# A hybrid encoder step: an empty step in the mixers' schedule, and two up-projection operands queued behind the out-projection

## The chip, the cores and the metric

The kernel runs on one core of one Trainium2 chip. The core has five engines, each with its own in-order queue: TensorE (PE) multiplies matrices, VectorE (DVE) and ScalarE (ACT) do elementwise work, GpSimd (POOL) does small elementwise work, and SyncE (SP) issues transfers. The metric is the device time of one execution in microseconds (us). The time before is the median of three runs, 1380.83 us (1377.18 to 1381.84).

## The reference

One inference step of one layer: a token mixer with three groups of heads in parallel (GLA, HGRN2 and mLSTM), then a causal convolutional feed-forward network, each with RMS norms and a residual. There are 1024 new prompt frames and 32 frames of a running stream, width 1024, feed-forward width 2816, all in float32.

```python
def run_layer(x, st, ffn_buf, p):
    xn = rms_norm(x, g_mix_pre)
    proj = xn @ w_in                               # queries, keys, values, gates of 16 heads
    o_a, s_gla = gated_linear_scan(q, k, v, log_a, s_gla)     # 6 heads
    o_b, s_hg = gated_linear_scan(q2, k2, v2, log_f, s_hg)    # 5 heads
    h, (c, n, m) = mlstm_scan(q3, k3, v3, log_fm, ig, c, n, m)  # 5 heads
    cat = concat(norm(o_a) * silu(.), norm(o_b) * silu(.), norm(h) * sigmoid(.))
    x = x + rms_norm(cat @ w_out, g_mix_post)
    up = causal_dwconv(rms_norm(x, g_ffn_pre) @ w_up, ffn_buf)
    gate, val = split(up)
    return x + rms_norm((gelu(gate) * val) @ w_down, g_ffn_post)
```

`gated_linear_scan` is S_t = diag(a_t) S_{t-1} + k_t v_t^T, o_t = S_t^T q_t, computed in blocks of 64 frames: scores within a block, and a state carried from block to block.

## The kernel before

The frames are worked on in nine units: units 0 to 7 are 128 prompt frames each, unit 8 is the 32 frames of the running stream. The in-projection takes them in three groups: units 0 to 2, units 3 to 5, and units 6, 7 and 8. Every product of float32 operands is three products of rounded halves: an operand is cast on ACT to its high half (name ending in h), DVE subtracts it to get the low half (ending in l), and `mm3` (L101 to L103) multiplies high by high, low by high and high by low.

Nothing in the program is ordered by hand in the end. A planner goes through the traced instructions with a model of the engines, and puts on each engine's queue the instruction that is ready, the one traced first ahead of the others. `tc.high_priority(offset=n)` lets instructions count as traced n places earlier. `tc.issue_after(ins)` makes every instruction traced inside it stand behind `ins` on the queue of the same engine. The order in which the Python generators are advanced therefore sets the priorities.

There are two strands. The main strand is the in-projection of a group (`inproj`, 38 steps: three of norm transposes and first values, feature tiles, then 21 steps of value and gate blocks of about 24 matmuls each) or, at the end, the out-projection (`pipeline` over the units 0, 1, 2, 3, 8, 4, 5). The side strand is the `mixer` of the units of the group before (units 8, 6 and 7, in this order, beside the out-projection). `merge` advances the two: after main step i, side steps are taken until (i+1)·nside/nmain of them have been done (integer division).

A mixer has nine steps, each ended by a `yield`: loads (eleven transfers into buffers of which there is mostly one); decays, scaled queries and keys; three steps of a pair of score levels each, the scores going from PSUM (sc) into the matrix P on DVE (`put`, L805), the last of these also with the state update (`states`, S, L902 and L903); the outputs (og and oh, 88 small matmuls for a full unit: P times v and the scaled queries qz times the states, then the memory update C); the output norm (`finish`, L987 to L992); the memory outputs om and oi, whose PSUM buffers are the same two as those of og and oh; and the norm of those, the gate and the store of the unit's 1024 columns (cat). `NMIX` sets how many side steps the merges count on: 3·NMIX − 6 beside the second group, 3·NMIX beside the third, 3·NMIX + 2 over 26 main steps of the out-projection.

At the end, the out-projection of units 6 and 7 overlaps the first up-projection block. `outproj` transposes a unit's columns (ctp, L1074), casts the halves of 512 columns to ch and cl (L1078, L1079; three buffers each), multiplies them with the weights (zp), takes z out of PSUM (L1101, L1102), norms it and adds the residual (L1147 to L1164), and transposes it again for the up-projection (fxt, L1178). ch waits for one of its three buffers, so the second half of unit 7 waits for the first products of unit 6. The up-projection multiplies 2x2 blocks by a scheme with seven products. Its column operands come from the loaded tile xg in `col_operands` (L1211): B21, B11 at once, and B12, B22 and their sums T1 to T4 after unit 5's columns have come. `halves` (L1216) makes each operand's two halves (L1221 on ACT, L1222 on DVE). The tiles of B21 and B11 lie in memory that the mixers have used. `kept` is a dictionary in which instructions are kept by name for later `issue_after`.

Of the kernel before, what the change touches and what calls it, by code (L numbers as in the profile page):

```python
# [8 lines left out]
F32 = mybir.dt.float32  # L9
# [4 lines left out]
ALU = mybir.AluOpType  # L14
# [77 lines left out]
def body(ctx: ExitStack, tc: tile.TileContext, a: dict):  # L92
    nc = tc.nc
    act, dve, pool, pe, sp = nc.scalar, nc.vector, nc.gpsimd, nc.tensor, nc.sync
# [620 lines left out]
    def soon(fn, *args, **kw):  # L715
        with tc.issue_after(line[0].ins) if line[0] else ExitStack():
            line[0] = fn(*args, **kw)  # L717

    def mixer(u, g, ci0):
# [3 lines left out]
        cl = chunks[0][1]  # L723
# [52 lines left out]
        with ExitStack() as behind:  # L776
            if halves:

                for ins in (kwi[0], halves[1]):
                    behind.enter_context(tc.issue_after(ins.ins))  # L780
            spread(dve, qz, lambda r, fs, psl: dve.tensor_tensor(qz[r, psl, :n], q4[r, fs, :], eb4[r, fs, :],
                                                                 op=ALU.mult), n)
# [3 lines left out]
        with tc.issue_after(outs[1].ins) if outs else ExitStack():  # L786
            dve.tensor_tensor(khf.rearrange("p (m c) -> p m c", c=cl), b5[:, :, cl - 1:cl].broadcast_to([128, 4 * nch, cl]),
                              b5, op=ALU.subtract)
# [55 lines left out]
        def scores(sc, c, L, Q, at):  # L844
            for j in (3, 0, 1, 2):
                for (o, m) in chunks:
                    for hf in range(2):
                        f, q0, q1, p0 = HALVES[hf][j]
                        r = slice(64 * hf, 64 * hf + 64)
                        mm = c if c == levels[0] else m  # L850
                        soon(pe.matmul, sc[o:o + mm, p0:p0 + q1 - q0, at:at + m // 2], L[r, f, o:o + mm],
                             Q[r, q0:q1, o // 2:(o + m) // 2], start=True, stop=True)
# [6 lines left out]
        def keys():  # L859
            for f0 in (0, 2):  # L860
                kps = small(2, 128)
                for f in (f0, f0 + 1):
                    soon(pe.transpose, kps[:n, f - f0, :], khf[:, f * n:f * n + n], ident)
                for ch, (o, m) in enumerate(chunks):
                    with tc.high_priority(offset=AHEAD):
                        act.copy(kt2[o:o + m, ch, 128 * f0:128 * f0 + 256], kps[o:o + m].rearrange("p f n -> p (f n)"))
# [4 lines left out]
        def memory_scores():  # L871
            sm = psm.tile([128, 6, 64], F32, tag="o", name=f"sm{u}", bufs=2)
            for f in range(3):
                rows, hs = (128, slice(2 * f, 2 * f + 2)) if f < 2 else (64, slice(4, 5))
                for (o, m) in chunks:
                    soon(pe.matmul, sm[o:o + m, hs, :m], mk[:rows, f, o:o + m], mqz[:rows, hs, o:o + m], start=True, stop=True)
            kp = small(4, 64)
            for f in range(2):
                soon(pe.transpose, kp[:n, 2 * f:2 * f + 2, :].rearrange("p h d -> p (h d)"), mk[:, f, :], ident)
            soon(pe.transpose, sm[:n, 5, :], mk[:64, 2, :], ident[:64, :64])  # L880
            for (h0, h1, kp) in ((0, 4, kp), (4, 5, sm[:, 5:6])):
                for ch, (o, m) in enumerate(chunks):
                    kwi[0] = dve.tensor_tensor(kw2[o:o + m, ch, h0:h1], kp[o:o + m, :h1 - h0],
                                               cols[o:o + m, 96 + h0:96 + h1].unsqueeze(2).broadcast_to([m, h1 - h0, 64]), op=ALU.mult)
            dve.tensor_tensor(w3, w3, sm[:n, :5, :cl], op=ALU.mult)
# [39 lines left out]
        for l0 in range(0, len(levels), 2):  # L925
            pair = [operands(c, i) for i, c in enumerate(levels[l0:l0 + 2])]
            last_pair = pair[-1][0] == levels[-1]
            if last_pair:
                z = mx.tile([128, 512], F32, tag="x", name=f"x{u}_0", bufs=NX)
                dve.tensor_tensor(z[:, :4 * n], q4.rearrange("p f n -> p (f n)"), k4.rearrange("p f n -> p (f n)"), op=ALU.mult)  # L930
            if l0 == 2:
                act.copy(mqz[0:64, 0:5:2, :n], mq[0:64, :, :])
                act.copy(mqz[64:128, 1:4:2, :n], mq[64:128, 0:2, :])
                dve.tensor_tensor(w3, ab3[:n], cols[:n, 0:5].unsqueeze(2).broadcast_to([n, 5, cl]), op=ALU.add)
                dve.tensor_tensor(w3, w3, caus[:n, :cl].unsqueeze(1).broadcast_to([n, 5, cl]), op=ALU.min)
                act.activation(w3, w3, AF.Exp)
            sct = psm.tile([128, 1024], F32, tag="sc", name=f"sc{u}_{l0}", bufs=1)
            sc = sct[:, :11 * SCW].rearrange("p (h s) -> p h s", s=SCW)
            line[0] = None
            for i in reversed(range(len(pair))):  # L940
                scores(sc, *pair[i], i * (cl // 2))
            sd = sct[:, 11 * SCW:11 * SCW + 11]
            if l0 == 0:
                keys()
            elif l0 == 2:
                memory_scores()
            if last_pair:
                for f in range(4):
                    soon(pe.matmul, sd[:n], z[:, f * n:f * n + n], of_head[:, f, :], start=f == 0, stop=f == 3)
                si = states()  # L950
            for i, (c, L, Q) in enumerate(pair):
                at = i * (cl // 2)
                if c == levels[0]:
                    for (o, m) in chunks:
                        act.copy(P[o:o + c, :, c:2 * c], sc[o:o + c, :, at:at + c])
                else:
                    put(c, sc[:n, :, at:at + cl // 2])
            if last_pair:
                put(0, sd[:n].unsqueeze(2).broadcast_to([n, 11, cl]))
            yield  # L960

        og = psm.tile([128, 6, 64], F32, tag="o", name=f"og{u}", bufs=2)
        oh = psm.tile([128, 5, 64], F32, tag="o", name=f"oh{u}", bufs=2)
# [90 lines left out]
    def outproj(p2, W, u):  # L1054
# [9 lines left out]
        for hf in range(2):  # L1064
            if u < 7 or u == 8:
                ps = psb.tile([128, 4, 128], F32, tag="big", name=f"ctp{u}{hf}")
            else:

                if not hf:
                    both = psm.tile([128, 2, 4, 128], F32, tag="sc", name="ctp7", bufs=1)  # L1070
                ps = both[:, hf]
            for k in range(4):
                c = 512 * hf + 128 * k
                pe.transpose(ps[:, k, :n], ct[:n, c:c + 128], ident[:n, :n])  # L1074
            ch = p2.tile([128, 4, 128], F32R, tag="ch", name=f"ch{u}{hf}", bufs=3)
            cl = p2.tile([128, 4, 128], F32R, tag="cl", name=f"cl{u}{hf}", bufs=3)
            with tc.high_priority(offset=AHEAD):
                ins = (act.copy(ch[:, :, :n], ps[:, :, :n]),  # L1078
                       dve.tensor_tensor(cl[:, :, :n], ps[:, :, :n], ch[:, :, :n].bitcast(F32), op=ALU.subtract))  # L1079
            if u == RING[0]:  # L1080
                halves[:] = ins
            chs += [(ch[:, k, :n], cl[:, k, :n]) for k in range(4)]
            if u in RING:
                yield
# [84 lines left out]
        else:  # L1169
            s = u > 5  # L1170
# [18 lines left out]
    upper, jks, kept = [], [], {}  # L1189
# [21 lines left out]
    def col_operands(pool_, q, s, between=lambda: None):  # L1211

        n = SUBS[s][1]
        res = {}

        def halves(name, src):  # L1216
            p = pool_[name in ("T2", "T3")]
            h = p.tile([128, 4, n], F32R, name=f"{name}h{s}")
            l = p.tile([128, 4, n], F32R, name=f"{name}l{s}")
            res[name] = h, l  # L1220
            act.copy(h, src)  # L1221
            return dve.tensor_tensor(l, src, h.bitcast(F32), op=ALU.subtract)  # L1222

        halves("B21", q["B21"])
        halves("B11", q["B11"])
        between()
        t1 = q["B11"]
        dve.tensor_tensor(t1, q["B12"], t1, op=ALU.subtract)
        halves("T1", t1)
        halves("B22", q["B22"])  # L1230
        t3, t2, t4 = q["B12"], q["B22"], q["B21"]
        dve.tensor_tensor(t3, q["B22"], t3, op=ALU.subtract)
        dve.tensor_tensor(t2, t2, t1, op=ALU.subtract)
        dve.tensor_tensor(t4, t2, t4, op=ALU.subtract)
        with ExitStack() as behind:
            if s == 0:
                behind.enter_context(tc.issue_after(kept["jk"].ins))
            halves("T2", t2)
        ins = halves("T4", t4)
        between()  # L1240
        with tc.issue_after(ins.ins):
            halves("T3", t3)
        return res
# [447 lines left out]
        return chain_of(*[mixer(u, g, c) for (u, c) in us[-1:] + us[:-1]]) if us[-1][0] == 8 else \  # L1691
            chain_of(*[mixer(u, g, c) for (u, c) in us])

    NMIX, NIN = 11, 12 + 2 + 24

    for g in range(3):
        xs_ = norm_tiles(g)
# [18 lines left out]
    n0, n1 = SUBS[0][1], SUBS[1][1]  # L1716
    smp = DEC // 2
    firsts = [outproj(p2, wo, u) for u in RING]
    merge(pipeline(firsts), 26, 3 * NMIX + 2)
    pump(1000)  # L1720
# [10 lines left out]
    p4s, p5s, p6s, p7s, p8s, p9s, pxs, phs, late = (ExitStack() for _ in range(9))  # L1731
# [213 lines left out]
```

## Time and profile before

| | before |
|---|---|
| median of three runs | 1380.83 us |
| the profiled execution, its time | 1379.03 us |
| the profiled execution, its span in the trace | 1377.3 us |
| mean granted TensorE clock | 0.982 |
| PE busy | 1313.3 us (95%) |
| DVE busy | 1031.8 us (75%) |
| ACT busy | 703.9 us (51%) |
| POOL busy | 325.6 us (24%) |

The span is divided into about 110 us of in-projection with no mixer beside it, the in-projections of the second and third group with the mixers of the group before to about 510 us, the out-projection with the last three mixers to about 680 us, the up-projection to about 1140 us, and the down-projection.

How to read the rows: a row of the timeline has the start and the duration in us, the engine, the line of the kernel, the operation, the output and the inputs by the program's names, their shapes, the number of merged instructions, and in brackets how long the engine was idle before and what ended the idle time. `SPq` and `POOLq` are queues that issue transfers. The granted clock is the share of TensorE's full clock.

### The profile page before, as it was taken

What the parts mean: (1) busy time and instruction counts of PE and PEld (TensorE: products, weight loads), DVE (VectorE), ACT (ScalarE), POOL (GpSimd) and SP (SyncE); (2) the same over time, 40 slices, a digit from 0 to 9 for tenths busy, and PEclk for the clock granted to TensorE, in tenths of its full rate; (3) what the DMA queues carried; (4) which work ended last, traced back from release to release, by engine and by line L of the source; (5) the groups of instructions that cost most, each with busy time, mean ns of one, the idle gap of its engine ahead of it and who ended that gap; (6) DMA issues with size and microseconds to landing.
All of it is one profiled execution on the core that took longest, in us unless ns stands there. A gap on an engine that the chain in (4) does not pass through costs nothing.

```text
span 1377.3 us, 29190 instructions
## 1 busy us (share of the span) xinstructions
PE 1313.3 (95%) x11472; PEld 1194.7 (87%) x11472; DVE 1031.8 (75%) x1916; ACT 703.9 (51%) x1368; POOL 325.6 (24%) x529
## 2 busy tenths in 40 slices
PE   6999999998998989997989999999999999999996
PEld 5999989998887877866879999999999997678885
DVE  4786469668597577796778888888888875499566
ACT  4555556554474554443575455455555445454552
POOL 5532403145122064133111112121121110010005
PEclk9999999999999999999999999999999999999998
DMA  9599869785888844534323565645474239744435
GB/s 343 203 321 359 288 235 299 267 281 188 273 256 309 303 147 161 155 114 151 110 77 110 170 165 135 163 129 163 111 182 126 81 114 390 290 153 136 146 106 123
DMA packets 125825, 269.72 MB, mean 196 GB/s; under 512 B 24007, under 2 KB 59367, under 8 KB 125607
## 3 DMA queue, kind: packets, MB, share of 16 engines
q1 hardware_dynamic: 111959, 245.43, 52.2%
q0 software_dynamic: 8928, 18.09, 7.2%
q10 hardware_dynamic: 4800, 4.33, 0.9%
q8 instruction: 90, 1.47, 0.4%
q14 instruction: 48, 0.39, 0.1%
HBM read 206.72 MB, written 86.18 MB: 213 GB/s over the span
## 4 chain that ended last, share of the span: by engine, by line
PE 72%; DVE 11%; DMA 7%; ACT 5%; issue 2%; POOL 2%; SPq 1%; ACTq 0%; DVEq 0%; POOLq 0%
PE pux L103 5%; PE pux L101 5%; PE pux L102 5%; PE puw L101 3%; PE puw L102 3%; PE puw L103 3%; PE pv L101 3%; PE pv L103 3%; PE q L101 3%; PE pv L102 3%; PE q L102 3%; PE q L103 3%; PE x L101 2%; PE x L102 2%; PE x L103 2%
## 5 line engine op out<-in xcount | busy, mean ns | idle before, releaser
L1368 DVE SCALAR_TENSOR_TENSOR y<-uu,fconv_sb,y 128x1060 f32<-128x1060 f32 x88 | 116.2, 1320 | 37.3 <-ACT y L1366 36.9
L1304 ACT COPY c<-pux 128x272 f32<-128x272 f32 (+1 forms) x132 | 49.4, 376 | 48.3 <-PE pux L103 47.6
L101 PE MATMUL zp<-woh,ch 128*128 128x512 f32 (+1 forms) x144 | 60.5, 422 | 4.8 <-ACT ch L1078 2.8
L101 PE MATMUL pv<-wt_0h,xh 128*128 128x256 f32 (+2 forms) x195 | 57.6, 296 | 5.2 <-ACT xh L321 2.8
L103 PE MATMUL zp<-woh,cl 128*128 128x512 f32 (+1 forms) x144 | 59.0, 410 | 1.9 <-DVE cl L1079 1.9
L1366 ACT ACTIVATE y<-uu,fconv_sb 128x1060 f32<-128x1060 f32 x44 | 56.0, 1273 | 7.9 <-POOL uu L1362 6.8
L102 PE MATMUL zp<-wol,ch 128*128 128x512 f32 (+1 forms) x144 | 58.9, 409 | 0.0
L1365 POOL COPY fhalo<-uu 128x2 f32<-128x2 f32 x44 | 16.5, 376 | 178.9 <-DVE uu L1309 178.7
L103 PE MATMUL pv<-wt_0h,xl 128*128 128x256 f32 (+2 forms) x195 | 56.0, 287 | 0.2 <-DVE xl L322 0.2
L102 PE MATMUL pv<-wt_0l,xh 128*128 128x256 f32 (+2 forms) x195 | 56.0, 287 | 0.1
L103 PE MATMUL pv<-wt_1h,xl 128*128 128x256 f32 (+2 forms) x195 | 56.1, 288 | 0.0
L101 PE MATMUL pv<-wt_1h,xh 128*128 128x256 f32 (+2 forms) x195 | 55.9, 287 | 0.0
L102 PE MATMUL pv<-wt_1l,xh 128*128 128x256 f32 (+2 forms) x195 | 55.7, 286 | 0.0
L1544 POOL TENSOR_TENSOR gss<-gss 128x1 f32<-128x1 f32 (+1 forms) x9 | 8.4, 930 | 185.1 <-ACT gjk L1537 185.1
L220 POOL TENSOR_SCALAR hrs<-hss 128x5 f32<-128x5 f32 (+3 forms) x27 | 9.7, 358 | 175.4 <-DVE hss L988 174.7
L805 DVE COPY_PREDICATED P<-masks_sb,sc 128x352 f32<-128x352 int32 (+3 forms) x53 | 37.8, 714 | 11.6 <-PE sc L717 10.9
L101 PEld LDWEIGHTS pv<-wt_0h,xh 128*128 128x128 f32 (+1 forms) x195 | 36.8, 189 | 7.1 <-ACT xh L321 3.5
L431 POOL TENSOR_TENSOR vg<-vth,gh 128x256 f32<-128x256 f32 (+1 forms) x36 | 29.1, 810 | 58.5 <-DVE vth L427 36.6
L221 POOL TENSOR_TENSOR hrs<-hrs,mhalf 128x5 f32<-128x5 f32 (+3 forms) x27 | 39.7, 1471 | 2.2
L827 ACT ACTIVATE x<-x 128x256 f32<-128x256 f32 (+1 forms) x44 | 17.9, 406 | 43.3 <-DVE x L825 36.1
L101 PEld LDWEIGHTS zp<-woh,ch 128*128 128x128 f32 (+1 forms) x144 | 27.4, 190 | 12.5 <-ACT ch L1078 3.0
L992 POOL TENSOR_TENSOR cat<-cat,gt 128x320 f32<-128x320 f32 (+3 forms) x27 | 31.7, 1174 | 26.4 <-DVE cat L990 26.3
(1714 smaller groups left out, 5351.3 us busy)
## 6 DMA issues: line engine op xcount, KB each, us to landing
wrP<-in_w_dn SPq DMA_DIRECT2D x27, 512.0 KB, 4.0
h_d<-y SPq DMA_DIRECT2D x22, 530.0 KB, 3.2
ht<-h_d SPq DMA_DIRECT2D x22, 530.0 KB, 9.8
wt_0r<-in_w_tok SPq DMA_DIRECT2D x21, 512.0 KB, 7.1
wt_1r<-in_w_tok SPq DMA_DIRECT2D x21, 512.0 KB, 6.1
ws_d<-in_w_dn POOLq DMA_DIRECT2D x20, 512.0 KB, 9.1
wrP<-ws_d SPq DMA_DIRECT2D x20, 512.0 KB, 3.9
wt_0l<-lt_d SPq DMA_DIRECT2D x14, 512.0 KB, 5.7
```

The costliest lines, as they stand in the source:

```text
L101: pe.matmul(ps, lh[0], rh[0], start=first, stop=False, **kw)
L102: pe.matmul(ps, lh[0], rh[1], start=False, stop=False, **kw)
L103: return pe.matmul(ps, lh[1], rh[0], start=False, stop=last, **kw)
L221: pool.tensor_tensor(out, out, mhalf[:n, :cols], op=ALU.pow)
L431: pool.tensor_tensor(o[:n], th[:n], gh[:n, c0:c0 + 256], op=ALU.mult)
L805: dve.copy_predicated(dst, mk.broadcast_to([n, 11, *mk.shape[2:]]), src)
L827: act.activation(xv[:, :, 0, :], xv[:, :, 0, :], AF.Exp, scale=-1.0)
L992: pool.tensor_tensor(cat[:n, c0:c0 + 64 * nh], cat[:n, c0:c0 + 64 * nh], gt[:n, c0:c0 + 64 * nh], op=ALU.mult)
L1304: kept[name] = act.copy(t, ps)
L1365: behind["POOL"] = pool.tensor_copy(fhalo[:, j, :], u[:, NCOL - 2:NCOL])
L1366: act.activation(y, u, AF.Identity, scale=fconv[:, j, 2:3], bias=fconv[:, j, 3:4])
L1368: dve.scalar_tensor_tensor(y, uu[i][:, s:s + NCOL], fconv[:, j, s:s + 1], y, op0=ALU.mult, op1=ALU.add)
```

## The change

The mixer gets a tenth step with nothing in it, between the last pair of score levels with the state update and the outputs; `NMIX` goes from 11 to 12, so that the side steps in the three merges become 30 (of 30), 36 (for 30) and 38 (for 30) in place of 27 (of 27), 33 (for 27) and 35 (for 27). And in `col_operands` for the first column half (s = 0), the two casts and the two subtractions that make the halves of B21 and B11 are put behind the cast and the subtraction of the last half of unit 7's out-projection operands, on ACT and DVE.

```diff
@@ mixer
             if last_pair:
                 put(0, sd[:n].unsqueeze(2).broadcast_to([n, 11, cl]))
             yield
+        yield
 
         og = psm.tile([128, 6, 64], F32, tag="o", name=f"og{u}", bufs=2)
@@ outproj
             if u == RING[0]:
                 halves[:] = ins
+            if u == 7:
+                kept["ch"], kept["cl"] = ins
             chs += [(ch[:, k, :n], cl[:, k, :n]) for k in range(4)]
@@ col_operands
             res[name] = h, l
-            act.copy(h, src)
-            return dve.tensor_tensor(l, src, h.bitcast(F32), op=ALU.subtract)
+            with ExitStack() as late:
+                if s == 0 and name in ("B21", "B11"):
+                    late.enter_context(tc.issue_after(kept["ch"].ins))
+                    late.enter_context(tc.issue_after(kept["cl"].ins))
+                act.copy(h, src)
+                return dve.tensor_tensor(l, src, h.bitcast(F32), op=ALU.subtract)
@@ body
-    NMIX, NIN = 11, 12 + 2 + 24
+    NMIX, NIN = 12, 12 + 2 + 24
```

The loop over the two halves of unit 7 keeps the instructions of the second half, which overwrite those of the first.

## The prediction

> **What bounds the kernel now.** I read the page's busy times first, then TensorE's own waits, then the stretches around those waits, and last the order of the engines where the out-projection hands over to the up-projection.
>
> ```profile
> PE 1313.3 (95%) x11472; PEld 1194.7 (87%) x11472; DVE 1031.8 (75%) x1916; ACT 703.9 (51%) x1368; POOL 325.6 (24%) x529
> ```
>
> TensorE (PE) is busy 1313.3 of 1377.3 us, and it has enough independent products to work on at almost every moment. So the time can move by two things only: idle time of PE, and stretches in which PE runs at a lower granted clock. The change removes no arithmetic. PE's waits, by who ended them (total, times, longest):
>
> ```profile
> PE og L717 <- DVE P L805: 5.2, 3, 2.8
> PE pb L455 <- ACT vf L468: 3.9, 2, 3.2
> PE zp L101 <- ACT ch L1078: 2.8, 1, 2.8
> PE om L717 <- DVE cat L990: 2.7, 2, 1.8
> PE zp L103 <- DVE cl L1079: 1.9, 1, 1.9
> ```
>
> The first and fourth rows are a mixer's output products (og) waiting for the score matrix P, and its memory outputs (om) waiting for a PSUM buffer that the output normalisation frees. The third and fifth rows are one place, the start of unit 6's out-projection. No row of that view has PE waiting for a DMA. The clock is in the stretches (columns: stretch, length, busy time and count of PE, weight loads, DVE, ACT, POOL, then granted clock, DMA share, GB/s):
>
> ```profile
> 190.00:200.00 10.00, 10.00 (x142) 8.58 (x141) 6.28 (x10) 6.95 (x9) 0.00 (x0) 0.83 0.67 249
> 312.00:322.00 10.00, 7.19 (x126) 6.80 (x126) 7.66 (x13) 3.32 (x9) 3.52 (x6) 0.83 0.29 100
> 436.00:448.00 12.00, 7.89 (x58) 7.00 (x57) 10.26 (x26) 6.12 (x14) 6.09 (x6) 0.72 0.91 352
> 654.00:659.00 5.00, 5.00 (x13) 3.95 (x13) 4.46 (x7) 1.63 (x3) 1.00 (x2) 0.52 0.51 137
> 645.00:667.20 22.20, 17.03 (x74) 13.35 (x73) 16.73 (x23) 10.30 (x18) 5.31 (x7) 0.85 0.41 123
> ```
>
> A stall therefore costs its idle time and, often, half-clock work beside it: 10 us at 0.83 is 1.7 us of work lost, 5 us at 0.52 is 2.4 us.
>
> **Part 2 of the change, the handover.** These are the rows of ACT, DVE, POOL and PE around it, in each engine's order (start, duration, what, idle before it and its releaser):
>
> ```profile
> 647.30 1.10 ACT L1221 CAST B21h<-xg 128x1088 fp32r<-128x1088 f32 x1 [3.56 <-POOL cat L992]
> 648.31 0.59 ACT L1101 ACTIVATE z<-zp 128x512 f32<-128x512 f32 x1
> 648.89 1.09 ACT L1221 CAST B11h<-xg 128x1088 fp32r<-128x1088 f32 x1
> 650.36 1.57 ACT L1078 CAST ch<-ctp 128x512 fp32r<-128x512 f32 x3
> 646.25 1.28 DVE L1183 TENSOR_TENSOR z<-fxt,gcols_sb 128x512 f32<-128x512 f32 x2
> 648.44 1.29 DVE L1222 TENSOR_TENSOR B21l<-xg,B21h 128x1088 fp32r<-128x1088 f32 x1 [0.91 <-ACT B21h L1221]
> 650.01 1.29 DVE L1222 TENSOR_TENSOR B11l<-xg,B11h 128x1088 fp32r<-128x1088 f32 x1 [0.28 <-ACT B11h L1221]
> 651.75 1.28 DVE L1154 SCALAR_TENSOR_TENSOR z<-z,oss,gm 128x1024 f32<-128x1024 f32 x1 [0.44 <-POOL oss L221]
> 652.95 1.88 DVE L1079 TENSOR_TENSOR cl<-ctp,ch 128x512 fp32r<-128x512 f32 x3
> 646.41 0.86 POOL L992 TENSOR_TENSOR cat<-cat,gt 128x320 f32<-128x320 f32 x1 [0.60 <-DVE cat L990]
> 649.07 0.71 POOL L1147 TENSOR_TENSOR oss<-oss 128x1 f32<-128x1 f32 x1 [1.80 <-ACT z L1101]
> 650.15 1.56 POOL L221 TENSOR_TENSOR oss<-oss,mhalf 128x1 f32<-128x1 f32 x1
> 644.82 0.40 PE L103 MATMUL zp<-woh,cl 128*128 128x512 f32 x1
> 646.99 1.26 PE L1074 MATMUL ctp<-ident,ct 128*128 128x128 f32 x8 [0.46 <-DVE z L1183]
> 651.01 0.50 PE L101 MATMUL zp<-woh,ch 128*128 128x512 f32 x1 [2.76 <-ACT ch L1078]
> 653.69 0.80 PE L103 MATMUL zp<-woh,cl 128*128 128x512 f32 x1 [1.94 <-DVE cl L1079]
> ```
>
> B21h stands at the head of ACT's queue and waits 3.56 us, until POOL has finished the last mixer (its tile lies in the memory that the mixers give back). Behind it stand the two leave operations of unit 5 (z, L1101 and L1102) and the three casts ch, for which the transposes end at 646.99 + 1.26 = 648.25. The edit takes the two casts (1.10 and 1.09 us) from in front of ch, and the two subtractions (1.29 each) from in front of cl on DVE. It issues no new instruction.
>
> Without them the leave operations go at about 645.2, when unit 5's products end, and unit 6's first cast runs while its second half is still transposed: PE's 2.76 us go. For cl there are two orders. If cl is put ahead of L1154 (cl is traced with priority), DVE is free at 646.25 + 1.28 = 647.5 and the first cl needed ends at about 649: PE starts the third product there instead of at 653.69, a gain of 4.7, all of 2.76 + 1.94. If L1154 stays ahead, it waits for POOL's chain (649.07 to 651.71, so 2.64 us), which can start only after L992 ends at 647.27: 649.9, plus 1.28 for L1154, plus two casts of 1.88/3: third product at 652.5, gain 1.2. I take 4.0, nearer the priority. The clock term, 2.4 us in 654–659, goes with the wait or stays with it: I take 2.0 (0 to 2.4).
>
> What is late next: B21 and B11 must follow the last halves of unit 7's operands.
>
> ```profile
> 662.38 0.59 ACT L1078 CAST ch<-ctp 128x512 fp32r<-128x512 f32 x1 [3.23 <-PE ctp L1074]
> 663.00 0.69 DVE L1079 TENSOR_TENSOR cl<-ctp,ch 128x512 fp32r<-128x512 f32 x1 [1.23 <-ACT ch L1078]
> 667.16 0.29 PE L101 MATMUL puy<-B21h,A_0h 128*128 128x272 f32 x1
> 668.84 0.48 PE L101 MATMUL zp<-woh,ch 128*128 128x512 f32 x1
> 679.61 0.39 PE L103 MATMUL zp<-woh,cl 128*128 128x512 f32 x1
> ```
>
> These last halves are ready at 663.69. Behind them the casts end at 664.1 and 665.2, the subtractions at about 665.3 and 666.6, just before PE wants them at 667.16. All of that moves earlier together, since ch waits for unit 6's first products. Queued behind the two delayed casts on ACT, and the two subtractions on DVE, can be weight halves S_0 of the first up-projection block; PE needs them for products after the ones with B21 and B11. DVE has 22.2 − 16.7 = 5.5 us idle in 645–667.2 for the 2.6 us, and behind 667.16 lies the cover: unit 7's 48 products, 668.84 to 679.61, 0.23 us each, 11 us. I cost it at nothing. Without that cover it costs the two subtractions, 2.6 us. Part 2: −4.0 − 2.0 = **−6.0** (−7.1 to +1.4).
>
> **Part 1, the empty step.** It issues nothing. It only changes which step of the main work each mixer step is traced behind, which is the planner's priority. Counting (i+1)·n/38 for the two in-projections and (i+1)·n/26 for the out-projection, with n from 27, 33, 35 to 30, 36, 38: the last score pair with the states comes one main step earlier in units 0, 1, 2 and 4; the outputs come one step later in units 2, 3, 5 and 7; unit 7's outputs no longer share a step with its states. Besides, these move by one: earlier unit 0's first pair, unit 1's loads and second pair, and unit 2's second step; later the output norms of units 0, 5, 6, 7, the memory outputs of 1, 4, 5, 8, the closing of unit 4, the loads of unit 5 and the second step of unit 7. An output step carries its products og and oh, the memory update's products and six DVE operations; an output norm two ACT, four DVE and six POOL instructions; a load step eleven SP transfers; unit 7's outputs one more, moved past the load of unit 5's rows. What stands on the path is only what PE waits for:
>
> ```profile
> 311.74 1.75 DVE L307 SCALAR_TENSOR_TENSOR x<-x,rs,gx 32x1024 f32<-32x1024 f32 x1 [0.70 <-POOL rs L221]
> 313.42 2.86 DVE L805 COPY_PREDICATED P<-masks_sb,sc 128x352 f32<-128x352 int32 x3
> 316.33 0.92 PE L717 MATMUL og<-v,P 64*64 64x64 f32 x24 [2.81 <-DVE P L805]
> 429.85 0.33 PE L717 MATMUL og<-v,P 64*64 64x64 f32 x4 [1.45 <-DVE P L805]
> 443.88 1.35 PE L717 MATMUL om<-vm,w 64*64 64x65 f32 x20 [0.89 <-DVE cat L990]
> 626.54 0.91 PE L717 MATMUL og<-v,P 64*64 64x64 f32 x24 [0.93 <-DVE P L805]
> 632.35 0.80 PE L717 MATMUL om<-vm,w 64*64 64x65 f32 x20 [1.83 <-DVE cat L990]
> ```
>
> Unit 2 (316.33): P is late because the three L307 operations of the next group stand ahead of it on DVE. With the states a step earlier, P is traced before them; with the outputs a step later, PE gets a step of 24 products in front of og. A 128x512 product takes 0.23 us, so 24 of half the columns are an estimated 2.8 us, as long as the wait of 2.81. I take 4.0 of 2.81 + 1.7 (clock). Unit 4: 1.45 + 0.89, both with a step more of room, I take 1.5. Unit 7: 0.93 has more room, but 1.83 is a wait for the norm, which itself moves a step later; I take 0.5. Against it, new waits. The nearest row is the longest wait of PE in the same stage, pb for vf, 3.2 us, with 12 × 0.28 = 3.4 us of clock in 436–448, so 0 to 6.6; I take 2. Part 1: −4.0 − 1.5 − 0.5 + 2.0 = **−4.0** (−9 to +7).
>
> Sum: −10.0. The profiled execution took 1379.03 us (span 1377.3 and 1.7 around it), so 1369.0; the median shown, 1380.83, is 1.8 higher, so **1370.8**.
>
> **The rivals.** *The clock stays.* In 190–200 PE is busy the whole 10 us and still has 0.83: there the states' and scores' small products run, and no gap. If the half-clock stretches come from those and not from the waits, they stay, and 2.0 + 1.7 is not gained: 1374.5. The row of 312–322 speaks against it, with its gap of 2.81. The Trainium skill (TensorE: Matmul & The Clock Gate, "Why this matters for your kernels") asks only that no idle gap exceed about 3 us; by it no gap of 2.81 or 2.76 costs clock, and the sum would also be 1374.5. The trace does not agree with it at 190–200, where the clock falls without a gap.
>
> *Nothing but a trade.* The planner orders everything anew; what units 2, 4 and 7 gain comes back elsewhere, and cl stays behind L1154: −1.2, so 1379.6. For it: the waits are spread over the whole mixer stage. Against it: the handover's cause is local.
>
> *Slower: v is held longer, and the weights with it.*
>
> ```profile
> SPq L739 <- PE oh L717: 32.9, 6, 9.5
> ```
>
> v has one buffer, and its next load waits in SP's queue for oh, up to 9.5 us already; the in-projection's weight loads stand behind it. Outputs a step later (units 2, 3, 5, each with a successor) hold that queue an estimated 2.8 us longer each. It decides once the hold exceeds the lead of the weight loads. Then PE loses 3 × (2.8 + 1.7) = 13.5 instead of gaining 4.0, and keeps part 2's 6.0: +7.5, so 1388.3. Against it: PE now waits for no DMA.
>
> **How the numbers follow.** Forecast 0.50, clock stays 0.13, trade 0.12, slower 0.25. A run of this kernel tells 0.3% from no change, 4.1 us: 1376.7 to 1385.0. Faster: 0.50 + 0.13 + 0.02 of the trade = 0.65; same: 0.10 + 0.02 of the slower case = 0.12; slower 0.23. The forecast's own range is 1361 to 1377; with most of the slower case, 1360 to 1389.
>
> **What would show it.** Right: no B21h ahead of ch at the handover, the two zp waits below 1.5 us together, 654–659 near clock 1.0; og's wait for P gone in unit 2; puy without a wait for B21l. Wrong: a new PE wait over 2 us for a DMA or for P in the mixer stage, or puy waiting for B21l after unit 7's products.

## The result, and the profile after

| | before | after |
|---|---|---|
| median | 1378.82 us (15 runs, 1373.37 to 1385.35) | 1374.32 us (15 runs, 1371.81 to 1378.15) |
| ratio after / before | | 0.9968 (0.9954 to 0.9982) |
| the profiled execution, its time | 1379.03 us | 1371.81 us |
| mean granted clock of the profiled execution | 0.982 | 0.987 |

The ratio is worth 0.0032 × 1378.82 = 4.4 us (2.5 to 6.3). The two profiled executions lie 7.2 us apart, because the one of after is the fastest of its 15 runs; so stretches are compared below, and not whole spans.

The changed kernel's page (span, then busy time, share and instructions of each engine):

```profile
span 1370.0 us, 29214 instructions
PE 1309.2 (96%) x11472; PEld 1191.7 (87%) x11472; DVE 1030.3 (75%) x1916; ACT 704.6 (51%) x1368; POOL 329.9 (24%) x529
```

The counts are those of before: nothing was added or removed. TensorE's waits in the changed kernel:

```profile
PE pb L455 <- ACT vf L468: 4.4, 1, 4.4
...
PE pv L101 <- DVE vth L427: 3.6, 2, 2.9
PE om L717 <- DVE cat L991: 3.2, 2, 1.8
...
PE og L717 <- DVE P L805: 2.1, 2, 1.1
...
PE zp L103 <- DVE cl L1080: 1.3, 1, 1.3
```

The wait of og for P fell from 5.2 to 2.1 us, and zp's for ch from 2.8 to 0.2; but pb waits 4.4 in place of 3.9, and pv for vth 3.6, with a longest of 2.9. The handover in the changed kernel, as the timeline has it for PE, ACT, DVE and POOL:

```profile
642.92 0.60 PE L1075 MATMUL ctp<-ident,cat 128*128 128x128 f32 x4
645.31 0.50 PE L101 MATMUL zp<-woh,ch 128*128 128x512 f32 x1 [0.24 <-ACT ch L1079]
647.30 0.50 PE L103 MATMUL zp<-woh,cl 128*128 128x512 f32 x1 [1.26 <-DVE cl L1080]
659.99 0.29 PE L101 MATMUL puy<-B21h,A_0h 128*128 128x272 f32 x1
660.11 1.04 PE L1181 MATMUL fxt<-ident,z 128*128 128x128 f32 x8
671.90 0.29 PE L102 MATMUL puy<-B21l,A_0h 128*128 128x272 f32 x1
...
642.25 0.60 ACT L1104 ACTIVATE z<-zp 128x512 f32<-128x512 f32 x1 [1.52 <-PE zp L103]
644.67 1.56 ACT L1079 CAST ch<-ctp 128x512 fp32r<-128x512 f32 x3 [1.11 <-PE ctp L1075]
656.81 1.11 ACT L1228 CAST B21h<-xg 128x1088 fp32r<-128x1088 f32 x1
...
645.36 1.28 DVE L1157 SCALAR_TENSOR_TENSOR z<-z,oss,gm 128x1024 f32<-128x1024 f32 x1 [0.84 <-POOL oss L221]
646.56 1.28 DVE L1080 TENSOR_TENSOR cl<-ctp,ch 128x512 fp32r<-128x512 f32 x2
659.16 1.28 DVE L1229 TENSOR_TENSOR B11l<-xg,B11h 128x1088 fp32r<-128x1088 f32 x1
...
644.22 0.20 POOL L1150 TENSOR_TENSOR oss<-oss 128x1 f32<-128x1 f32 x1
644.78 0.55 POOL L221 TENSOR_TENSOR oss<-oss,mhalf 128x1 f32<-128x1 f32 x1
```

Lines have moved by one to three (L1078 is L1079, L1154 is L1157). ACT goes from the leave operations straight to ch; B21h comes 12 us later, and the first puy products take B21h and B21l without a wait. Unit 5's norm multiply, L1157, still stands ahead of cl on DVE, and cl's wait is 1.26 us. The two waits together are 0.24 + 1.26 = 1.50, where they were 2.76 + 1.94 = 4.70.

The clock of the changed kernel from the start of unit 6's transposes (ctp) to the transposes of z (fxt), and over the first 5 us from the first low product on (columns as in the prediction's windows):

```profile
642.90:660.10 17.20, 15.25 (x67) 11.92 (x66) 14.55 (x20) 9.38 (x17) 2.49 (x6) 0.90 0.51 154
647.30:652.30 5.00, 5.00 (x15) 3.96 (x16) 4.16 (x6) 2.81 (x5) 0.35 (x2) 0.66 0.94 301
```

The start of the transposes in the kernel before, and its clock over the 5 us from the first low product on:

```profile
645.93 0.60 PE L1074 MATMUL ctp<-ident,cat 128*128 128x128 f32 x4
653.69:658.69 5.00, 5.00 (x12) 3.98 (x13) 4.77 (x7) 1.42 (x4) 0.69 (x2) 0.50 0.44 113
```

To compare the same work in both, take the stretch from the start of unit 6's transposes to the first product puy: 645.93 to 667.16 before, which is 21.23 us, and 642.92 to 659.99 after, which is 17.07. So this place became 4.2 us shorter. Of these, 3.2 are waits. From the first low product to puy there is no idle time of PE in either kernel, and that part fell from 13.47 to 12.69 us: 0.8 of clock. The remaining 0.2 is the transposes, 1.26 and 1.09 us.

### The profile page after: what moved, and what is told of

It reads as the page before. It is cut to its first block, busy times and chain, and to the rows that moved or that the text cites. A ratio compares the mean times of both kernels' runs of the same rounds, so it can differ in the third digit from the quotient of the medians.

```text
span 1370.0 us, 29214 instructions
## 1 busy us (share of the span) xinstructions
PE 1309.2 (96%) x11472; PEld 1191.7 (87%) x11472; DVE 1030.3 (75%) x1916; ACT 704.6 (51%) x1368; POOL 329.9 (24%) x529
## 4 chain that ended last, share of the span: by engine, by line
PE 65%; DVE 13%; DMA 8%; ACT 7%; issue 3%; POOL 3%; SPq 1%; ACTq 0%; DVEq 0%; POOLq 0%
PE pux L103 5%; PE pux L102 5%; PE pux L101 5%; PE puw L102 3%; PE puw L103 3%; PE puw L101 3%; PE q L101 3%; PE q L102 3%; PE q L103 3%; PE pv L101 3%; PE pv L103 2%; PE x L101 2%; DMA qkb<-qkb_d 2%; PE pv L102 2%; PE x L102 2%
## 5 line engine op out<-in xcount | busy, mean ns | idle before, releaser
L1369 POOL COPY uu<-uu 128x2 f32<-128x2 f32 x44 | 31.4, 714 | 43.6 <-DVE uu L1316 42.7
L221 POOL TENSOR_TENSOR hrs<-hrs,mhalf 128x5 f32<-128x5 f32 (+3 forms) x27 | 39.3, 1454 | 2.3
L102 PEld LDWEIGHTS pv<-wt_0l,xh 128*128 128x128 f32 (+1 forms) x195 | 36.9, 189 | 0.6 <-POOL wt_0l L110 0.5
```

Of the source, the lines that this page charges most:

```text
L102: pe.matmul(ps, lh[0], rh[1], start=False, stop=False, **kw)
L221: pool.tensor_tensor(out, out, mhalf[:n, :cols], op=ALU.pow)
L1369: pool.tensor_copy(u[:, GAP_P:GAP_P + 2], u[:, GAP_S - 2:GAP_S])
```

## The experiments

Two theories were tested first. One: the handover carries the whole gain, and the empty step only moves waits about. Its rival: both parts gain, the step about as much as the handover. All kernels ran in two sets of five rounds, each set on one chip beside the kernel before (1378.68 us there in the first set, 29 runs; 1379.74 in the second, 18 runs).

**The empty step alone.**

```diff
+        yield
-    NMIX, NIN = 11, 12 + 2 + 24
+    NMIX, NIN = 12, 12 + 2 + 24
```

> The empty step with NMIX 12 alone; B21 and B11 are queued as before. Theory A (the handover carries the gain, the empty step mostly trades waits): 0 to -3 us against before, ratio 0.998 to 1.000, and at the start of unit 6's products the two waits for ch and cl are there as before, 4 to 5 us together. Theory B (the step carries the gain): -4 us or more, ratio at most 0.997. Theory C (the two only work together): slower than before.

Measured: 1378.82 us (12 runs), ratio 1.0003 (0.9988 to 1.0018). TensorE's waits between 150 us and the handover (150 to 642 us), first in the kernel before:

```profile
PE og L717 <- DVE P L805: 5.2, 3, 2.8
...
PE pv L101 <- DVE vth L427: 0.8, 2, 0.6
PE oi L717 <- DVE cat L990: 0.3, 1, 0.3
```

and with the step alone:

```profile
PE pv L101 <- DVE vth L427: 3.8, 1, 3.8
PE om L717 <- DVE cat L991: 3.1, 2, 1.8
PE oi L717 <- DVE cat L991: 2.9, 3, 1.1
...
PE og L717 <- DVE P L805: 0.9, 1, 0.9
...
PE mi L717 <- ACT kt L866: 0.6, 2, 0.4
```

og's wait for P falls by 4.3 us, as the change means it to. In its place pv's wait for vth grows from 0.8 to 3.8 us, and oi's for the norm from 0.3 to 2.9: the fifteen rows of each view add up to 25.0 us before and 26.0 with the step. The handover is as it was (zp waits 2.77 and 1.82), and PE comes to it at the same time: unit 6's transposes start at 646.04, against 645.93 before. The step is worth nothing that can be measured, though it does just what it says at og. A single profile tells such waits only roughly: the changed kernel has the same mixers, and by the same view its waits for P are 2.1 and not 0.9, its wait for vth 2.9, and its sum 25.7.

**The queueing alone.**

```diff
+            if u == 7:
+                kept["ch"], kept["cl"] = ins
...
+                if s == 0 and name in ("B21", "B11"):
+                    late.enter_context(tc.issue_after(kept["ch"].ins))
+                    late.enter_context(tc.issue_after(kept["cl"].ins))
```

> The queueing of B21 and B11 behind unit 7's last operands alone; nine mixer steps and NMIX 11 as before. Theory A: -4 to -5 us, ratio 0.996 to 0.997; the mixer stage up to 640 us has before's waits, 2.8 us before og at unit 2 among them; the two waits at unit 6 together are 1.5 us, and from there to the end the trace runs 4 to 5 us earlier than before. Theory B: 0 to -2 us, ratio at least 0.9985.

Measured: 1375.41 us (12 runs), ratio 0.9970 (0.9959 to 0.9982): the whole gain of the change. Its handover on PE:

```profile
649.77 0.50 PE L101 MATMUL zp<-woh,ch 128*128 128x512 f32 x1 [0.24 <-ACT ch L1078]
651.76 0.50 PE L103 MATMUL zp<-woh,cl 128*128 128x512 f32 x1 [1.26 <-DVE cl L1079]
662.82 0.29 PE L101 MATMUL puy<-B21h,A_0h 128*128 128x272 f32 x1
```

The waits are those of the changed kernel, and og's 2.8 us in unit 2 are there as before. The products behind ran at full clock in this profile: from the first low product to puy it is 651.76 to 662.82, which is 11.06 us against 13.47 before. The first theory holds.

**The change with the empty step elsewhere.** Its place is a parameter, so it was put ahead of the first pair of score levels (first run), and behind the output norm (second run), with the queueing kept:

```diff
+        yield          # first run: decays, this, first score pair
...
-        yield          # both runs: not ahead of og, oh
...
+        yield          # second run: output norm, this, memory outputs
```

> As the changed kernel, but the empty step stands after the decays and scaled keys, before the first score pair, in place of before the outputs; NMIX 12 the same. If the place before the outputs matters (the matrix P gets time), the waits of og for P are back, 5 us together as before, and the time is 2 to 4 us above the changed kernel, ratio about 0.999. If the step only reshuffles the planner's order, any place does as well: ratio 0.995 to 0.998.

Measured: 1382.79 us (12 runs), ratio 1.0029 (1.0014 to 1.0044), 8 us above the changed kernel, which neither theory had. TensorE's waits there:

```profile
PE zp L103 <- DVE cl L1080: 5.1, 2, 3.4
PE sc L717 <- issue: 4.7, 2, 4.0
PE pv L101 <- ACT vf L468: 4.1, 4, 2.7
...
PE ctp L1075 <- DVE z L1186: 2.7, 1, 2.7
```

In the changed kernel's list sc has no row for issue and pv none for vf; zp waits 1.3 for cl and ctp 0.5 for z. Why the scores and the transposes ctp come late there was not followed further.

> The change, with the empty step one place later: after the output norm, ahead of the memory outputs. Theory A (an empty step moves waits about and gains nothing; its place matters only where it makes the waits of PE longer, as it did ahead of the first score pair): og's wait of 2.8 us for P in unit 2 is back, as the outputs are no longer moved; time between 1373 and 1379 us, and the handover as in the changed kernel (about 4.4 us from the transposes to the first low product). Theory B (each step between the scores and the end of a unit gives room to P, and its place is what gains): 1375.5 to 1378 us, 1 to 4 us above the changed kernel, all of it og's wait. A loss beyond that (over 1379) speaks against both.

Measured: 1373.79 us (7 runs), ratio 0.9961 (0.9947 to 0.9974), no different from the changed kernel. Its waits between 310 and 325 us:

```profile
PE og L717 <- DVE P L805: 2.9, 1, 2.9
```

Unit 2's wait is back and costs nothing over the whole. So an empty step gains nothing ahead of the outputs or behind the norm, and loses ahead of the scores.

**Which of the two engines' queues held the handover.** Only the subtractions stand behind the last halves; the casts keep their place:

```diff
                 if s == 0 and name in ("B21", "B11"):
-                    late.enter_context(tc.issue_after(kept["ch"].ins))
                     late.enter_context(tc.issue_after(kept["cl"].ins))
```

> The change, but only the two subtractions on DVE stand behind the last halves of unit 7's operands; the casts B21h and B11h keep their old place on ACT, ahead of ch. Theory A (the gain comes from ACT, where B21h waits at the head of the queue for POOL's end of the last mixer): zp's wait for ch stays at about 2.8 us, the stretch from the start of unit 6's transposes to its first low product (7.76 us before, 4.38 in the changed kernel) stays above 6.5, the time is within 1.5 us of before (ratio 0.999 to 1.001). Theory B (the subtractions, 2 x 1.29 us in front of cl, carry about half): zp's wait for cl falls from 1.9 to below 0.7, the stretch comes to about 6, the ratio to about 0.9985.

Measured: 1376.06 us (10 runs), ratio 0.9981 (0.9971 to 0.9992). The handover (ACT, PE, POOL):

```profile
642.65 1.10 ACT L1227 CAST B21h<-xg 128x1088 fp32r<-128x1088 f32 x1 [3.57 <-POOL cat L993]
...
646.35 0.50 PE L101 MATMUL zp<-woh,ch 128*128 128x512 f32 x1 [2.77 <-ACT ch L1079]
647.84 0.80 PE L103 MATMUL zp<-woh,cl 128*128 128x512 f32 x1 [0.66 <-DVE cl L1080]
...
644.41 0.19 POOL L1150 TENSOR_TENSOR oss<-oss 128x1 f32<-128x1 f32 x1 [1.80 <-ACT z L1104]
644.97 0.55 POOL L221 TENSOR_TENSOR oss<-oss,mhalf 128x1 f32<-128x1 f32 x1
```

The wait for ch is whole, so it belongs to B21h on ACT; the wait for cl falls from 1.94 to 0.66, so that much of it belonged to the subtractions on DVE. The stretch from unit 6's transposes to the first low product is 6.55 us (641.29 to 647.84): each theory has one of the two waits right, and the time lies between them. By the ratios the subtractions alone give a bit over half of the gain (0.0019 of 0.0032), with intervals that overlap. The casts alone were not run, so ACT's share is known as the rest only. POOL's two operations are the ones to note: 644.41 to 645.52 is 1.1 us, against 649.07 to 651.71, 2.6 us, in the kernel before.

**What was left at the handover.** Unit 5's norm multiply behind unit 6's two subtractions cl, with unit 6's operands traced before that norm:

```diff
+            if u == 6:
+                kept["cl6"] = ins[1]
...
-            dve.scalar_tensor_tensor(z[:n], z[:n], ss[:n, 3:4], gm[:n], op0=ALU.mult, op1=ALU.mult)
+            with tc.issue_after(kept["cl6"].ins) if u == 5 else ExitStack():
+                dve.scalar_tensor_tensor(z[:n], z[:n], ss[:n, 3:4], gm[:n], op0=ALU.mult, op1=ALU.mult)
...
+            if not after:
+                next(last[0])
...
+    last = [outproj(p2, wo, u) for u in (6, 7)]
     merge(pipeline(firsts), 26, 3 * NMIX + 2)
     pump(1000)
-    last = [outproj(p2, wo, u) for u in (6, 7)]
-    for x in (last[0], last[0], last[1]):
+    for x in (last[0], last[1]):
```

> The changed kernel, and unit 5's norm multiply on VectorE stands behind the two cl subtractions of unit 6, which it is ahead of in the changed kernel. If that multiply is what is left of the wait for cl (1.26 us), the wait goes to 0.3 us or less and the time falls by 1 us, by up to 2.7 if the half-clock stretch behind it goes as well: ratio 0.994 to 0.996. If the subtraction waits for its own cast or transpose, the wait stays and nothing is gained.

Measured: 1370.72 us (6 runs), ratio 0.9941 (0.9922 to 0.9960). It was run once more, and also without the empty step:

> The change with unit 5's norm multiply behind unit 6's two subtractions cl, once more, beside the next kernel. Measured before: 1370.72 us, ratio 0.9941 (0.9922 to 0.9960). Theory A (what was left at the handover is a wait of 1.26 us for cl and the half clock behind it, 3.4 us): ratio 0.993 to 0.996 again, no wait of zp for ch or cl. Theory B (that value came from six lucky runs): ratio 0.9965 to 0.998, as with the queueing alone.

Measured: 1372.71 us (6 runs), ratio 0.9950 (0.9931 to 0.9968).

```diff
-        yield          # ahead of og, oh
...
-    NMIX, NIN = 12, 12 + 2 + 24
+    NMIX, NIN = 11, 12 + 2 + 24
```

> The kernel of the run before without the empty step (NMIX 11): the queueing and the norm multiply's place alone. Theory A (the empty step is worth nothing): the same time as with the step, ratio 0.993 to 0.996, og's wait of 2.8 us for P in unit 2 is there again and some waits of the changed kernel's mixer stage are gone. Theory B (the step gains its 2 to 4 us once the handover no longer hides it): slower than with the step by 2 to 4 us, ratio 0.9965 or more.

Measured: 1370.98 us (7 runs), ratio 0.9943 (0.9917 to 0.9970). As expected, og's 2.8 us in unit 2 are there again. The handover of this last kernel, on PE, and its clock over a stretch as long as that of the changed kernel:

```profile
642.83 0.60 PE L1074 MATMUL ctp<-ident,cat 128*128 128x128 f32 x4
643.86 1.09 PE L1183 MATMUL fxt<-ident,z 128*128 128x128 f32 x8 [0.43 <-ACT z L1106]
645.07 0.50 PE L101 MATMUL zp<-woh,ch 128*128 128x512 f32 x1
645.64 0.40 PE L103 MATMUL zp<-woh,cl 128*128 128x512 f32 x1
```

```profile
642.83:660.00 17.17, 16.62 (x86) 13.64 (x85) 15.65 (x22) 11.47 (x25) 2.81 (x6) 1.00 0.54 178
```

No product waits for ch or cl there, and the clock is whole. The edit moved more than the norm multiply, though: unit 6's transposes now stand ahead of unit 5's fxt on PE, and its 1.09 us lie between them and the first product. How much of the wait each of the two removes was not separated. The best kernels measured are the queueing with the norm multiply moved, with or without the step: 7 to 8 us below before by their ratios, and by the medians 2 to 4 below the changed kernel, which ran beside before on other occasions. The intervals of these ratios overlap with that of the change, so the further gain is likely and not shown. That the step doesn't matter was expected and shows here once more. The second half of the up-projection's columns is what is late next: its puy waits 2.62 us for B21h in this kernel. That was not tried.

## Why the prediction was right, and where it was not

The forecast of 1370.8 us lies 3.5 us below the median measured; the direction and the larger of its two parts are right, and its other part is wrong. That the time came so near is in part luck: of the 10.0 us forecast, 4.4 came, and the kernel before measured 2.0 us less over 15 runs than the 1380.83 that the forecast started from.

**Part 2, −6.0: the mechanism is right, a little too large.** In the profile the place gained 4.2 us, and the queueing alone measured 0.0030 × 1378.68 = 4.1 us (2.5 to 5.7). The term of the waits, −4.0, measured −3.2. It was taken nearer the case in which cl goes ahead of the norm multiply; the norm multiply stayed ahead. That other case had been priced at 1.2, too low by 2.0, for two reasons. It counted two casts of cl, 1.25 us, ahead of the product, where the row before shows that PE started 0.74 us after the first began (652.95 to 653.69). And it carried over POOL's 2.64 us before the norm multiply as if they were POOL's own work. They were not. In the kernel before, B21l (648.44 to 649.73) and B11l (650.01 to 651.30) ran beside POOL's two operations, which took 0.71 and 1.56 us; without them the same two take 0.20 and 0.55. So each subtraction moved cost twice, in DVE's queue and through POOL, on which the norm multiply ahead of cl waits. The run with only the subtractions moved shows it alone.

The clock term, −2.0, measured −0.8 in this profile and −2.4 in that of the queueing alone (13.47 to 11.06 us). The sentence that 654–659 would come near full clock is wrong for the profile of after (0.66 in the 5 us from the first low product on). The two waits, forecast below 1.5 together, stand at 1.50. B21 and B11 late cost next to nothing, as said: the only wait of puy, 0.4 us for B21h, was 0.6 before. Further on, puw waits 1.8 us for T1h and 1.3 for T1l, where it waited 1.9 for T1h and 0.9 for c.

**Part 1, −4.0: wrong.** The step measured 1.0003, that is between −1.7 and +2.5 us. The two terms for og did come: unit 2's 2.81 went, and og's waits for P fell by 4.3 us in the run of the step alone. The term that failed is the new waits, taken as 2 and measured, by the same view, as 5.3 (4.3 gone and the sum 1.0 higher), or as 3.8 in the changed kernel (3.1 gone and the sum 0.7 higher). The prediction had its bound, 6.6, and took a value from its lower half without a reason for it. The edit leaves a mixer's work as it was, and its engines serve it and the in-projection both; by the waits, what P gained, vth (3.8 us) and the norm of the outputs lost. Which operation stood ahead of vth on DVE was not followed.

The range has a slip too: its lower end of 1361 does not follow from the bounds of the two parts, since −7.1 and −9 from 1380.83 give 1364.7.

**The rivals.** *Nothing but a trade* was right of part 1 and of the place of cl, and wrong by the POOL term of the handover. *The clock stays* fell at the handover: the half-clock stretch of before is in every profile that keeps the wait for ch, and in none that has no wait there at all. The clocks are those of 5 us from the first low product on:

| kernel | waits of zp for ch and cl, us | granted clock behind them |
|---|---|---|
| before | 4.70 | 0.50 |
| the step alone | 4.59 | 0.54 |
| only the subtractions behind | 3.43 | 0.50 |
| the change | 1.50 | 0.66 |
| the queueing alone | 1.50 | 1.00 |
| the step behind the output norm | 1.50 | 1.00 |
| the step ahead of the first score pair | 1.88 | 0.61 |
| norm multiply moved (both runs), and without the step | 0 | 1.00 |

With the step ahead of the first score pair PE had waited 2.74 us before unit 6's transposes as well.

*Slower by v and SP's queue* fell the other way about. The row of SP's queue that the prediction shows for the kernel before is, in the changed kernel:

```profile
SPq L739 <- PE oh L717: 18.9, 5, 7.2
```

The hold by oh fell from 32.9 to 18.9 us. That is the step's doing: it is 18.5 with the step alone and 33.4 with the queueing alone. The hold of the next load in the same queue by om (L741) rose from 15.3 to 18.9. Why oh holds the queue for less was not followed. No wait of PE for a transfer appeared in the changed kernel.

## What to carry to other kernels

An operand whose memory is released late belongs behind the work that is due, on every in-order queue it passes: the one cast at the head of ACT's queue held three casts and two leave operations, and its subtraction held another engine besides. A wait removed from a stage in which the engines are shared by two strands was worth nothing here, because the sum of waits over the stage had not fallen; the waits removed at the handover, where one strand is left, were worth their length and some of the clock behind them. And when a chain is carried over from the profile of before, ask of each duration whether the work to be moved is what made it long.

## What the runs showed of the hardware

**POOL waits for some DVE operations.** POOL's operation on 128x1 (L221) takes 0.55 us beside nothing, and 0.55 beside the subtraction cl, which reads one input from PSUM (644.68 in the last kernel); it took 1.56 beside B11l, whose two inputs both lie in SBUF, and 1.54 in the changed kernel beside another such subtraction:

```profile
665.11 1.29 DVE L1229 TENSOR_TENSOR B22l<-xg,B22h 128x1088 fp32r<-128x1088 f32 x1 [0.25 <-ACT B22h L1228]
...
665.27 1.54 POOL L221 TENSOR_TENSOR oss<-oss,mhalf 128x1 f32<-128x1 f32 x1
```

Both times POOL's operation ends 0.41 us after the subtraction (665.27 + 1.54 against 665.11 + 1.29, and 651.71 against 651.30): it does not run slower, it waits for the end. The Trainium skill (SBUF — State Buffer, "Who interferes with whom") says that a VectorE instruction with two SBUF inputs contends with a GpSimd instruction that reads SBUF, and that the ports they share are an exclusive lock. The trace agrees for POOL behind DVE, with 1.56 and 1.54 us in place of 0.55. It does not show the lock the other way round: in the kernel before, the subtraction B22l started 0.08 us behind a POOL operation of 0.55 us (673.11 and 673.03) and took its usual 1.29.

**The clock is a matter of the run too.** Over the 15 runs of the changed kernel, time and mean granted clock go against each other with a correlation of −0.85: 1371.81 us at 0.987, 1378.15 at 0.979. The same two waits of 0.24 and 1.26 us were followed by a clock of 0.66 in one kernel's profile and of 1.00 in two. Likewise om's last wait, 1.83 us, had full clock behind it in the kernel before (1.00 in 633.65 to 638.65), and 1.82 us had 0.66 in the first run with the norm multiply moved (636.47 to 641.47). So a short wait puts clock at risk rather than costing it each time, while the two waits of 3.4 us together and more had 0.50 to 0.54 behind them in all three profiles that have them. The Trainium skill (TensorE: Matmul & The Clock Gate, "Why this matters for your kernels") sets the gap to avoid at about 3 us. In these profiles shorter gaps were followed by a low clock as well: 0.50 behind 2.76 and 1.94 us, and 0.66 behind 0.24 and 1.26. Whether the gap or the work around it is the cause there was not settled.
